# Eight chunks of the convolution's input, not four, projected during the first stage, with undivided fp32 weights

## The chip, the cores and the metric

One NeuronCore of a Trainium2 chip runs the whole program. The metric is the device time of one execution in microseconds (us), the median of the executions shown. The kernel is written in Bass with the Tile framework, which places the tiles, inserts the semaphores and orders the instructions of each engine.

## The reference

Two transformer-like blocks work on 256 tokens of width 2048. The change lies in the opening of the first block:

```python
mod = (cond @ ada_w + ada_b)                 # cond: 2048, ada_w: 2048 x 12288
sh1, sc1, g1, sh2, sc2, g2 = split(mod, 6)
h = rms_norm(x, norm_mix) * (1.0 + sc1) + sh1
proj = h @ w_in                              # q, kv, gates, z, xbc, dt
attn = nsa_attention(q, kv, gates, ...)      # 16 heads
xbc = silu(causal_depthwise_conv(xbc, conv_w, conv_b))   # 1536 channels
ssm = ssd_scan(xbc, dt, ...) * silu(z)
x = x + g1 * (concat(rms_norm(attn), ssm) @ w_out)
x = x + g2 * peer_ffn(...)
```

An entry of `sh1` or `sc1` needs all 2048 rows of its column of `ada_w`; the kernel reads these columns in four groups, so that `h` becomes ready quarter by quarter of its 2048 features.

## The kernel before, in words

**Layout.** Activations stand with the features on the partitions: 16 slices of 128 features, 256 tokens each. Weights come in tiles of 128 x 1024 fp32, 512 KB each. One chunk is 128 output columns of `w_in`; a pair of chunks is 256 columns. The 1536 channels of the convolution are 12 chunks, or 6 pairs.

**Split and whole.** A product in higher precision is made of three fp32r products: `wt` loads a weight tile into a `raw` buffer (L263: four buffers `raw` and two `rawm`) and divides it into `whi` (ScalarE, L281) and `wlo` (VectorE, L285); `mm3` (L298) multiplies high by high, high by low and low by high (L300, L301, L302). `whi` and `wlo` have two buffers each. `whole` (L290) instead loads a tile straight into a buffer of the tags `whi` or `wlo`, in turn, for one plain fp32 product; the compiler issues that as two TensorE instructions. Every one of these loads is issued on SP's queue.

**First stage.** A background generator (`mods`, L518) reads four groups of 16 tiles of `ada_w` (a quarter each; `ada`, L355) and accumulates each on VectorE (L364). After a quarter `mod` (L503) sums over the partitions on TensorE (L376), adds the bias (L508), and `chunks_T` turns four slices of `x` and writes them as `hh` and `hl`, the two parts of `h`. `early` (L561) is the foreground: for each quarter it takes 6 tiles for `kv` and `q`, accumulated over the four quarters in PSUM, and `NP` tiles for `NP` pairs of the convolution's chunks. A pair's sum over one quarter goes to a PSUM bank (tag `sm`, two banks in this stage) and is added to `part` in SBUF (L589, L591); after the last quarter `ev` of `ssd_front` applies the convolution. In quarters 0 to 2 the pairs are spread among the six, in quarter 3 they come last.

**Pacing.** `fill` (L1412) advances the foreground by one weight tile, and then the background by `bgr` steps, 16 / (NP + 5) here. `until` and `drain` call `fill` in a loop.

**Behind it.** `mixer` waits for the second `kv` tile, runs `compress` (with six calls of `fill` in it, at a `bgr` of 0.6), drains `early`, and feeds the queue with `t320` (6 tiles), the remaining chunks of the convolution (`cm`, L1338, two tiles each, `mm3`), and 16 tiles for `z`. `weave` (L1441) runs the 16 attention heads two at a time and calls `fill` at a rate of 0.28 a step. Behind the heads come 32 tiles of `w_out` (`tm_whole`, L1378, through `whole`) and the scan. Meanwhile the background reads 96 more tiles of `ada_w` (`ada_rest`, L606) at a `bgr` of 1.3; what is left of it is run off before the second half of the block.

Of the kernel before, what the change touches and what calls it, by code (L numbers as in the profile page):

```python
# [18 lines left out]
S = 256  # L19
NK = D // 128  # L20
EPS = 1e-6
LAG = 3
NP = 2

# [207 lines left out]
class K:  # L234
# [219 lines left out]
        if lo is not None:  # L454
            nc.vector.scalar_tensor_tensor(lo, ps, scale, hi.bitcast(F32), op0=ALU.mult, op1=ALU.subtract)

    def chunks_T(self, pool, x, cs, dg, hh, hl, scale, shift):

        nc = self.nc
        for c0 in range(cs[0], cs[-1], 2):  # L460
            v = self.t(pool, [128, 2, S], tag="cT", bufs=2 if dg is None else 4)
            ps = self.bank()
            for i in range(2):
                c = c0 + i
                o = ps[:, i * S : i * S + S]
                for q in range(2):
                    self.turn(o[:, q * 128 : q * 128 + 128], x[:, q, c * 128 : c * 128 + 128], None if dg is None else dg[:, q])
                if i:
                    nc.vector.tensor_scalar(v[:, i], o, scale[:, c : c + 1], shift[:, c : c + 1], op0=ALU.mult, op1=ALU.add)  # L469
                else:  # L470
                    nc.scalar.activation(v[:, i], o, AF.Identity, scale=scale[:, c : c + 1], bias=shift[:, c : c + 1])
            k = slice(c0, c0 + 2)
            self.hilo(hh[:, k], hl[:, k], v)

    def block1(self, upto=99):
        nc, tc, A = self.nc, self.tc, self.A
        con = self.con
        self.psum(6, 2)
        scr = tc.alloc_tile_pool(name="scr", bufs=1, space=DRAM)
        hp = self.hp = tc.alloc_tile_pool(name="hp", bufs=1)  # L480
        self.more = tc.alloc_tile_pool(name="more", bufs=1)
        mx = tc.alloc_tile_pool(name="mx", bufs=1)
        ax = tc.alloc_tile_pool(name="ax", bufs=1)
        xp = tc.alloc_tile_pool(name="xp", bufs=1, side="right")
        xt = self.t(xp, [128, 2, D])
        self.zeros = self.t(ax, [128, 128], F32R)
        nc.vector.memset(self.zeros.bitcast(F32), 0.0)
        self.cond = self.t(con, [128, 16])
        self.silu_small(con, self.cond, self.cp("c"), 16)
        modA = self.t(con, [128, 32])  # L490
        self.modB = self.t(con, [128, 32])
        hT = self.pair(hp, NK, "hh")
        hh, hl = hT[:2]
        cA = self.t(con, [128, 16])

        kvT = self.t(ax, [128, 4, S])
        qT = self.t(ax, [128, 8, S])
        xs, ev = self.ssd_front(mx)
        part = self.t(ax, [128, NP, 512])
        self.feed(self.early(A["w1e"], hT, kvT, qT, part, ev))  # L500
        quarter = lambda m, c: m.rearrange("p (m c j) -> p m c j", m=2, c=4)[:, :, c]

        def mod(acc, c):  # L503
            ps = self.bank()
            self.ada_mm(acc, ps[:, :8])
            yield
            p = ps[:, :8].rearrange("p (m j) -> p m j", m=2)
            nc.vector.tensor_tensor(quarter(modA, c), p, quarter(self.cp("ada_b")[:, :32], c), op=ALU.add)  # L508
            hs = slice(4 * c, 4 * c + 4)
            sc = slice(16 + 4 * c, 20 + 4 * c)  # L510
            nc.vector.scalar_tensor_tensor(cA[:, hs], modA[:, sc], 1.0, self.cp("norm_mix")[:, hs], op0=ALU.add, op1=ALU.mult)
            for i in range(2):
                k = 4 * c + 2 * i
                self.chunks_T(xp, xt, range(k, k + 2), None, hh, hl, cA, modA)
                yield
            self.done.add(("h", c))

        def mods():  # L518
            post = iter(())
            for c in range(4):  # L520
                acc = self.t(xp, [128, 1024], tag="ada", bufs=2)
                for _ in self.ada(acc, c):
                    yield
                    next(post, None)
                post = mod(acc, c)
            for _ in post:
                yield

        self.bg = [mods()]
        for _ in range(10):  # L530
            self.step_bg()
        for q in range(2):
            nc.sync.dma_start(xt[:, q], A["x"][q * 128 : q * 128 + 128])
        ss = self.t(xp, [128, 4])
        for n in range(4):
            junk = self.t(xp, [128, 2, S], tag="cT", bufs=2).rearrange("p a b -> p (a b)").bitcast(mybir.dt.bfloat16)
            x = xt[:, n // 2, n % 2 * 1024 : n % 2 * 1024 + 1024]
            nc.scalar.activation(junk, x, AF.Square, accum_out=ss[:, n : n + 1])
        sv = ss.rearrange("p (q h) -> p q h", h=2)
        nc.vector.tensor_tensor(sv[:, :, 0], sv[:, :, 0], sv[:, :, 1], op=ALU.add)  # L540
        r = self.rstd(xp, sv[:, :, 0], 2, float(D))
        for n in range(4):
            x = xt[:, n // 2, n % 2 * 1024 : n % 2 * 1024 + 1024]
            nc.scalar.activation(x, x, AF.Copy, scale=r[:, n // 2 : n // 2 + 1])
        for _ in range(6):
            self.step_bg()
        self.pack(mx, "cp2")
        self.pack(mx, "ca")
        self.bgr = 16 / (NP + 5)
        self.fill(8)  # L550
        self.bias_front(ax, scr)
        self.until(("h", 3))
        self.dbg("hh", hh.bitcast(F32))
        xp.release()
        hT = self.mixer(hp, mx, ax, hT, kvT, qT, xs, ev, scr)
        if upto < 4:
            hp.release()
            return
        return self.peer(hp, hT, upto)

    def early(self, wd, hT, kvT, qT, part, ev):  # L561

        nc = self.nc
        ps = [self.t(self.acc, [128, 512], tag="acc") for _ in range(6)]
        for p in ps:
            z = self.zeros[:, None, :].to_broadcast([128, 4, 128])
            nc.tensor.matmul(p, self.zeros, z, start=True, stop=False)
        for c in range(4):
            order = [*range(NP, NP + 6), *range(NP)]
            if c < 3:  # L570
                order.sort(key=lambda n: (n - NP) / 6 if n >= NP else (n + 0.5) / NP)
            for n in order:
                hi, lo = self.wt(wd[(NP + 6) * c + n])
                yield
                while ("h", c) not in self.done:
                    self.step_bg()
                pn = ps[n - NP] if n >= NP else self.bank()
                for i in range(2):
                    o = pn[:, i * 256 : i * 256 + 256]
                    for k in range(4):  # L580
                        sl = slice(i * 512 + k * 128, i * 512 + k * 128 + 128)
                        kk = 4 * c + k
                        if n >= NP:
                            self.mm3(o, hi[:, sl], lo[:, sl], hT[0][:, kk], hT[1][:, kk], False, kk == 15 and i == 1)
                        else:
                            self.mm3(o, hi[:, sl], lo[:, sl], hT[0][:, kk], hT[1][:, kk], k == 0, k == 3)
                if n < NP:
                    if c == 0:
                        nc.scalar.activation(part[:, n], pn, AF.Copy)  # L589
                    else:  # L590
                        nc.vector.tensor_tensor(part[:, n], part[:, n], pn, op=ALU.add)  # L591
                    if c == 3:
                        for i in range(2):
                            ev((2 * n + i + 8) % 12, part[:, n, i * 256 : i * 256 + 256])
                    continue
                if c < 3:
                    continue
                n -= NP
                o = pn.rearrange("p (a t) -> p a t", a=2)
                if n < 2:  # L600
                    nc.scalar.activation(kvT[:, 2 * n : 2 * n + 2], o, AF.Copy)
                else:
                    nc.scalar.activation(qT[:, 2 * n - 4 : 2 * n - 2], o, AF.Copy, scale=-0.125)
                self.done.add(("early", n))
# [10 lines left out]
    def mixer(self, hp, mx, ax, hT, kvT, qT, xs, ev, scr):  # L615
        nc, tc, A = self.nc, self.tc, self.A
        hh, hl = hT[:2]
# [35 lines left out]
        nc.scalar.activation(gate, vtm[:, :, 256:304], AF.Tanh, scale=0.5)  # L653
        nc.vector.tensor_scalar(gate, gate, 0.5, 0.5, op0=ALU.mult, op1=ALU.add)
        self.side.append(self.ssd_steps(mx, xs, vtm))
        at = self.t(ax, [128, 2, 1024])
        self.weave([self.head(ax, j, kv, qT, kvT, kc, vc, vtm, gate, at) for j in range(8) for kv in range(2)], 1, 0.28)
        self.dbg("attn", at)
        ss = self.t(ax, [128, 2])
        for q in range(2):  # L660
# [83 lines left out]
    def bias_group(self, ax, g):  # L744
# [4 lines left out]
        for kv in range(2):  # L749
            skew = bass.AP(tensor=ud.tensor, offset=ud.offset + 384 * (8 * kv + 2 * g), ap=[[1, 128], [384, 2], [1, 256]])  # L750
            nc.sync.dma_start(tf[:, 2 * kv : 2 * kv + 2], skew)
        tab = self.t(ax, [128, 4, 256], tag="tab", bufs=2)
        for i in range(2):
            ps = self.bank()
            nc.tensor.matmul(ps, flip, tf[:, 2 * i : 2 * i + 2], start=True, stop=True)
# [1583 lines left out]
```

## Time and profile before

| | |
|---|---|
| median of 3 executions | 3599.55 us (3596.58 to 3600.33) |
| profiled execution | 3600.31 us, its span 3598.2 us |
| mean granted TensorE clock | 0.979 of full speed |
| TensorE busy | 3427.4 us (95%) |
| VectorE, ScalarE busy | 2565.5 us (71%), 1632.8 us (45%) |
| DMA over the span | 710.40 MB, 197 GB/s |

The span is the time from the first to the last instruction of the profiled execution. A busy share is that of recorded instructions. TensorE's instructions overlap and their ends are modelled, so its pace is read from one start to the next, not from the durations.

### The profile page before, as it was taken

The page shows a single profiled execution, that of the slowest core. Times are in us where ns is not written, and L with a number is a line of the kernel's source. Part 1 is how long each engine was busy: PE and PEld are TensorE (multiplying, and loading weights), DVE is VectorE, ACT ScalarE, POOL GpSimd, SP SyncE. Part 2 cuts the span into 40 slices and gives each one's busy share as a digit, 9 for nine tenths or more (in the row PEclk, how much of TensorE's full clock was granted, in tenths as well). Part 3 has the DMA queues.
Part 4 walks back from the last instruction along what each step waited for, and adds up shares of the span by engine and source line. Part 5 has one row for each costly group of instructions (what it writes and reads, how often), then busy time and mean ns, then how long its engine had stood idle before and what let it go on. Part 6 is the DMA issues. An engine that isn't in the chain of part 4 may idle for free. (4 is left out here: it accounts for less than half of the span.)

```text
span 3598.2 us, 52389 instructions
## 1 busy us (share of the span) xinstructions
PE 3427.4 (95%) x18918; PEld 2852.2 (79%) x18918; DVE 2565.5 (71%) x4648; ACT 1632.8 (45%) x2934; POOL 390.3 (11%) x487
## 2 busy tenths in 40 slices
PE   5899999999999999999999998988999999999998
PEld 4888747888998888888878786776788888778887
DVE  7777666788887655565577658878777767666765
ACT  2355424444554444445555554333444444434444
POOL 0000010000000000000000002333223222021310
PEclk7999999999999999999999999999999999999999
DMA  9966785666456855566788765645533443434455
GB/s 345 333 222 206 266 290 177 199 198 201 159 162 208 257 185 186 187 203 205 240 271 287 254 206 186 203 160 180 169 113 113 150 138 108 134 123 159 146 182 186
DMA packets 237294, 710.40 MB, mean 197 GB/s; under 512 B 34091, under 2 KB 61804, under 8 KB 235756
## 3 DMA queue, kind: packets, MB, share of 16 engines
q1 hardware_dynamic: 207564, 672.08, 56.8%
q10 hardware_dynamic: 29472, 34.98, 2.9%
q8 instruction: 149, 2.44, 0.3%
q14 instruction: 109, 0.89, 0.1%
HBM read 673.87 MB, written 32.55 MB: 196 GB/s over the span
## 5 line engine op out<-in xcount | busy, mean ns | idle before, releaser
L285 DVE TENSOR_TENSOR wlo<-raw,whi 128x1024 fp32r<-128x1024 f32 (+1 forms) x951 | 1167.8, 1229 | 567.1 <-ACT whi L281 562.8
L281 ACT ACTIVATE whi<-raw 128x1024 fp32r<-128x1024 f32 (+1 forms) x951 | 994.0, 1046 | 1224.8 <-PE acc L302 577.3
L308 PE MATMUL acc<-hh,whi 128*128 128x512 f32 x3328 | 1197.9, 401 | 0.7 <-DVE cT L469 0.7
L309 PE MATMUL acc<-hh,wlo 128*128 128x256 f32 x3328 | 940.0, 282 | 7.1 <-DVE wlo L285 6.9
L308 PEld LDWEIGHTS acc<-hh,whi 128*128 128x128 f32 x3328 | 627.0, 188 | 145.6 <-issue 4.5
L309 PEld LDWEIGHTS acc<-hh,wlo 128*128 128x128 f32 x3328 | 629.6, 189 | 13.5 <-DVE wlo L285 12.0
L301 PE MATMUL acc<-wlo,wh 128*128 128x512 f32 x1024 | 402.1, 393 | 8.0 <-DVE wlo L285 7.2
L300 PE MATMUL acc<-whi,wh 128*128 128x512 f32 x1024 | 396.6, 390 | 3.5 <-DVE ge L1355 2.8
L302 PE MATMUL acc<-whi,wl 128*128 128x512 f32 x1024 | 399.3, 390 | 0.0
L301 PE MATMUL acc<-wlo,hh 128*128 128x512 f32 (+1 forms) x608 | 243.7, 401 | 14.9 <-DVE wlo L285 14.7
L300 PE MATMUL acc<-whi,hh 128*128 128x512 f32 (+1 forms) x608 | 248.1, 409 | 5.3 <-DVE r L1355 5.3
L302 PE MATMUL acc<-whi,hh 128*128 128x512 f32 (+1 forms) x608 | 242.1, 398 | 0.0
L301 PEld LDWEIGHTS acc<-wlo,wh 128*128 128x128 f32 x1024 | 192.5, 188 | 58.6 <-DVE wlo L285 18.8
L300 PEld LDWEIGHTS acc<-whi,wh 128*128 128x128 f32 x1024 | 192.3, 188 | 45.7 <-ACT wh L281 3.1
L302 PEld LDWEIGHTS acc<-whi,wl 128*128 128x128 f32 x1024 | 192.7, 188 | 38.9
L302 PE MATMUL acc<-hh,wlo 128*128 128x256 f32 x608 | 181.7, 299 | 27.9 <-DVE wlo L285 27.9
L300 PE MATMUL acc<-hh,whi 128*128 128x256 f32 x608 | 182.3, 300 | 5.4 <-ACT whi L281 3.4
L301 PE MATMUL acc<-hh,whi 128*128 128x256 f32 x608 | 178.5, 294 | 1.0 <-DVE hh L285 1.0
L301 PEld LDWEIGHTS acc<-wlo,hh 128*128 128x128 f32 x608 | 118.3, 195 | 43.1 <-DVE wlo L285 21.1
L302 PEld LDWEIGHTS acc<-hh,wlo 128*128 128x128 f32 x608 | 122.0, 201 | 34.0 <-DVE wlo L285 31.9
L1819 POOL TENSOR_TENSOR r<-r,cb 128x256 f32<-128x256 f32 x144 | 129.7, 920 | 163.7 <-DVE r L2149 38.1
L364 DVE SCALAR_TENSOR_TENSOR ada<-raw,u,ada 128x1024 f32<-128x1024 f32 x101 | 131.7, 1304 | 21.6 <-DMA raw<-in_ada_dram 20.7
(591 smaller groups left out, 4913.8 us busy)
## 6 DMA issues: line engine op xcount, KB each, us to landing
raw<-in_pu_dram SPq DMA_DIRECT2D x256, 512.0 KB, 3.6
raw<-in_pv_dram SPq DMA_DIRECT2D x252, 512.0 KB, 4.2
raw<-in_ada_dram SPq DMA_DIRECT2D x139, 512.0 KB, 5.2
raw<-in_w2gate_dram SPq DMA_DIRECT2D x96, 512.0 KB, 3.6
rawm<-in_ada_dram SPq DMA_DIRECT2D x53, 512.0 KB, 5.5
raw<-in_w2br_dram SPq DMA_DIRECT2D x48, 512.0 KB, 3.5
raw<-in_w2g_dram SPq DMA_DIRECT2D x48, 512.0 KB, 3.5
raw<-in_wq_dram SPq DMA_DIRECT2D x32, 512.0 KB, 3.6
```

The lines of the kernel that those rows point to most:

```text
L281: nc.scalar.activation(hi, src, AF.Copy)
L285: self.lo = e.tensor_sub(lo, src, hi.bitcast(F32)).ins
L300: mm(out, shi, mhi, start=start, stop=False)
L301: mm(out, shi, mlo, start=False, stop=False)
L302: mm(out, slo, mhi, start=False, stop=stop)
L308: mm(out, hi, both, start=start, stop=False)
L309: mm(out[:, S:], lo, both[:, 0], start=False, stop=stop)
L364: nc.vector.scalar_tensor_tensor(acc, w, c, acc, op0=ALU.mult, op1=ALU.add)
L1819: PL.tensor_tensor(v2(lb), v2(L), cb(f"M{b}"), op=ALU.mult)
```

## The change

`NP` goes from 2 to 4. The pairs no longer use `wt` and `mm3`: their weight tile is loaded by `whole`, and multiplied in plain fp32 with an undivided `h`, which `chunks_T` now leaves in a tile `v` for a whole quarter. That tile takes a buffer of the tag `tab` (three buffers now, two before; the attention's bias tables use the same tag later), and `part` shares its buffer with `at`, the attention's output. `w1cm`, the array for `cm`, has 8 tiles fewer, `w1e` 8 more. `bgr` in the first stage becomes 16/9 from 16/7, and the rate in `weave` goes from 0.28 to 0.23.

```diff
-NP = 2
+NP = 4
...
-    def chunks_T(self, pool, x, cs, dg, hh, hl, scale, shift):
+    def chunks_T(self, pool, x, cs, dg, hh, hl, scale, shift, v=None):
...
-            v = self.t(pool, [128, 2, S], tag="cT", bufs=2 if dg is None else 4)
+            if dg is not None:
+                v = self.t(pool, [128, 2, S], tag="cT", bufs=4)
...
-        part = self.t(ax, [128, NP, 512])
-        self.feed(self.early(A["w1e"], hT, kvT, qT, part, ev))
+        part = self.t(ax, [128, 2048], tag="at").rearrange("p (n t) -> p n t", n=NP)
+        parts = {}
+        self.feed(self.early(A["w1e"], hT, parts, kvT, qT, part, ev))
...
+            v = parts[c] = self.t(ax, [128, 4, S], tag="tab", bufs=3)
...
-                self.chunks_T(xp, xt, range(k, k + 2), None, hh, hl, cA, modA)
+                self.chunks_T(xp, xt, range(k, k + 2), None, hh, hl, cA, modA, v[:, 2 * i : 2 * i + 2])
...
-                hi, lo = self.wt(wd[(NP + 6) * c + n])
+                if n < NP:
+                    w = self.whole(wd[(NP + 6) * c + n])
+                else:
+                    hi, lo = self.wt(wd[(NP + 6) * c + n])
...
-                            self.mm3(o, hi[:, sl], lo[:, sl], hT[0][:, kk], hT[1][:, kk], k == 0, k == 3)
+                            nc.tensor.matmul(o, w[:, sl], parts[c][:, k], start=k == 0, stop=k == 3)
...
-        at = self.t(ax, [128, 2, 1024])
-        self.weave([...], 1, 0.28)
+        at = self.t(ax, [128, 2048], tag="at").rearrange("p (q c) -> p q c", q=2)
+        self.weave([...], 1, 0.23)
...
-        tab = self.t(ax, [128, 4, 256], tag="tab", bufs=2)
+        tab = self.t(ax, [128, 4, 256], tag="tab", bufs=3)
```

## Rows read from the trace of the kernel before

**Rows 1.** The page: span, and DMA share in tenths in 40 slices.

```profile
span 3598.2 us, 52389 instructions
...
DMA  9966785666456855566788765645533443434455
```

**Rows 2.** Stages: length, busy time (instructions) per engine, clock, DMA share, GB/s.

```profile
36.50:69.50 33.00, 25.82 (x170) 23.23 (x169) 28.78 (x29) 9.13 (x11) 0.00 (x0) 0.81 0.95 344
69.50:105.70 36.20, 27.91 (x196) 24.86 (x195) 30.94 (x32) 10.07 (x12) 0.00 (x0) 0.95 0.90 331
105.70:141.10 35.40, 28.32 (x194) 26.98 (x192) 31.11 (x32) 9.59 (x11) 0.00 (x0) 0.86 0.97 350
141.10:182.00 40.90, 37.72 (x279) 35.91 (x277) 24.02 (x29) 16.88 (x22) 0.00 (x0) 0.92 0.89 301
182.00:224.30 42.30, 40.91 (x287) 37.74 (x287) 29.87 (x46) 18.83 (x31) 0.40 (x4) 0.92 0.75 253
224.30:314.00 89.70, 89.42 (x657) 79.94 (x656) 72.59 (x233) 52.82 (x166) 5.12 (x16) 0.98 0.62 193
314.00:403.20 89.20, 89.20 (x500) 73.27 (x500) 64.64 (x187) 45.48 (x144) 4.68 (x8) 0.92 0.61 197
```

**Rows 3.** Line L508, the bias behind each of the four quarters.

```profile
L508 DVE TENSOR_TENSOR u<-sm,cp x4: 166/167/168, 36.5 to 141.1; 128x8 f32<-128x8 f32 x4
```

**Rows 4.** Line L267 from 36.5 to 141.1 us: SP's issues and landings.

```profile
L267 SPq DMA_DIRECT2D raw<-in_ada_dram x30: 327/328/332, 40.3 to 137.6; - x30
L267 SPq DMA_DIRECT2D raw<-in_w1e_dram x15: 327/328/351, 38.0 to 136.4; - x15
L267 SPq DMA_DIRECT2D rawm<-in_ada_dram x14: 327/328/383, 38.7 to 129.4; - x14
L267 SPq DMA_DIRECT2D rawm<-in_w1e_dram x9: 327/328/328, 51.7 to 138.9; - x9
...
DMA to landing us min/median/max: 3.6/5.3/7.0
```

**Rows 5.** Timeline of TensorE: first matmuls of two adjoining divided tiles.

```profile
151.27 0.28 PE L300 MATMUL acc<-hh,whi 128*128 128x256 f32 x1
...
154.09 0.28 PE L300 MATMUL acc<-hh,whi 128*128 128x256 f32 x1
```

**Rows 6.** Timeline of TensorE from 504 to 562 us, whole tiles of `w_out`.

```profile
504.76 3.60 PE L1387 MATMUL acc<-whi,hh 128*128 128x512 f32 x8
508.19 0.60 PE L441 MATMUL sm<-cs,u 128*128 128x128 f32 x4
...
560.82 1.40 PE L376 MATMUL sm<-ones,ada 128*128 128x1 f32 x12
```

**Rows 7.** Timeline of SP: issue of a `w1e` tile.

```profile
122.63 0.33 SPq L267 DMA_DIRECT2D raw<-in_w1e_dram  x1
```

**Rows 8.** Timeline of VectorE: a division, a `part` sum.

```profile
130.37 1.22 DVE L285 TENSOR_TENSOR wlo<-raw,whi 128x1024 fp32r<-128x1024 f32 x1 [1.03 <-ACT whi L281]
...
134.58 0.69 DVE L591 TENSOR_TENSOR u<-u,sm 128x512 f32<-128x512 f32 x1 [0.47 <-PE sm L302]
```

**Rows 9.** Timeline of SP from 504 to 545 us.

```profile
504.95 0.33 SPq L295 DMA_DIRECT2D wlo<-in_wo_dram  x1
505.37 0.38 SPq L267 DMA_DIRECT2D raw<-in_ada_dram  x1
508.39 0.33 SPq L295 DMA_DIRECT2D whi<-in_wo_dram  x1
...
541.21 0.91 SPq L267 DMA_DIRECT2D raw<-in_wq_dram  x2
```

**Rows 10.** Timeline of VectorE: the background's last sum.

```profile
549.50 1.28 DVE L364 SCALAR_TENSOR_TENSOR ada<-raw,u,ada 128x1024 f32<-128x1024 f32 x1
```

**Rows 11.** A stage of `w_out` and the scan; columns as in rows 2.

```profile
416.00:436.00 20.00, 20.00 (x76) 11.44 (x76) 13.57 (x19) 7.25 (x17) 0.00 (x0) 1.00 1.02 406
```

More of the change, by code (lines that the diff above doesn't have):

```diff
@@ L559, in block1, with early @@
         return self.peer(hp, hT, upto)
-    def early(self, wd, hT, kvT, qT, part, ev):
+    def early(self, wd, hT, parts, kvT, qT, part, ev):
         nc = self.nc
@@ L655, in mixer @@
         self.side.append(self.ssd_steps(mx, xs, vtm))
-        at = self.t(ax, [128, 2, 1024])
-        self.weave([self.head(ax, j, kv, qT, kvT, kc, vc, vtm, gate, at) for j in range(8) for kv in range(2)], 1, 0.28)
+        at = self.t(ax, [128, 2048], tag="at").rearrange("p (q c) -> p q c", q=2)
+        self.weave([self.head(ax, j, kv, qT, kvT, kc, vc, vtm, gate, at) for j in range(8) for kv in range(2)], 1, 0.23)
         self.dbg("attn", at)
```

## The prediction

> **What bounds the kernel now.** I read the page first, for its DMA line: the first two of 40 slices, each 90 us of the span, are the only ones in which the DMA engines are at nine tenths [rows 1]. The table of stages then shows that the opening has two parts with different limits [rows 2]. In the first, which I bound by the bias of quarters 0 and 3 at 36.5 and 141.1 us [rows 3], the DMA share is 0.90 to 0.97 and TensorE has records in only about 77 to 80% of the time, although each record's end is stretched by the model. In the second, from 182 us on, TensorE is full and the DMA share falls to 0.75 and, under the attention heads (224.3 to 403.2 us), to 0.61. So work moved from behind the heads' start into the first part trades TensorE time for DMA time. The stretch between, 141.1 to 224.3 us, belongs to neither: TensorE is at 92 to 97%, at a granted clock of 0.92, and DMA at 0.75 to 0.89.
>
> Line L267 gives the first part's pace [rows 4]: 30 + 15 + 14 + 9 = 68 tiles issued in 104.6 us, 1.54 us each, and a median of 5.3 us from issue to landing, so some 3.4 tiles are in flight.
>
> Two more prices. A divided tile (24 matmuls of 256 columns) takes TensorE 154.09 - 151.27 = 2.82 us [rows 5]. A plain fp32 tile is not in this stage, but the tiles of `w_out` are: eight instructions of 512 columns, 508.19 - 504.76 = 3.43 us [rows 6]. A pair's tile is 16 instructions of 256 columns, the same number of columns with the same pass over each, so I take 3.43 us.
>
> **The change part by part.** *TensorE's total.* Removed: 8 divided tiles of the two old pairs in the first stage and 8 divided tiles of four chunks in `cm`, 16 x 2.82 = 45.1 us. Added: 16 whole tiles, 16 x 3.43 = 54.9 us. The sum rises by 9.8 us, so the change can only gain by filling time in which TensorE idles. Where this falls matters.
>
> *First part, up to quarter 3's bias.* The counters of the code fix how many `w1e` tiles are issued before `h` is complete: the background needs 68 steps, 20 are done by the second `fill`, and 48 / (16/7) = 21 further ones follow, 22 tiles of 32. With 16/9 it is 48 / (16/9) = 27, 28 tiles of 40. Six more tiles at 1.54 us are +9.2 us if DMA stays the limit. TensorE would carry about 17 divided and 11 whole tiles there, 48 + 38 = 86 us, with the turns and sums (some 10 us) under 100 of 114 us: it has room. VectorE loses eight divisions of 1.22 us in the whole stage and gains six sums of 0.69 us [rows 8]: room too (90.8 us busy of 104.6 before, [rows 2]).
>
> *The whole tile's wait.* This is new. `whole` writes into a `whi` or `wlo` buffer, so SP may issue it only when TensorE is done with that buffer's last tile, and behind it on SP's queue stand all the `raw` loads, the `ada_w` tiles among them. I followed the two buffers of each tag through the order kv/q, pair, kv/q, kv/q, pair, q, pair, q, q, pair: pairs 0 and 2 of a quarter wait for the tile three places back, pairs 1 and 3 for the one two places back. From issue to the end on TensorE a divided tile takes 130.37 - 122.63 = 7.7 us to the start of `wlo`, 1.22 for it and 2.82 of matmuls, 11.8 us [rows 7, 8, 5]. Places are 114 / 28 = 4.1 us apart. Three places (12.2 us) need no wait; two (8.1 us) make SP wait about 3.7 us. That the queue really goes in step with TensorE in such a case is seen at `w_out`: SP issues whole tiles at 504.95 and 508.39, each 0.2 us behind a step of TensorE at 504.76 and 508.19, and the `ada_w` loads only behind them [rows 9, 6]. The cover is what is in flight: 5.3 us. While it lasts, a 3.7 us wait costs DMA nothing; without it the full 3.7 us. Six such waits: 0 to 22 us. I take 2.5 us, near the covered end, since the wait is shorter than the flight.
>
> *Middle part, up to the heads.* Before, 10 divided tiles are left (28.2 us). After, 12: the last divided one and the last pair of quarter 2, then six divided and four whole, 7 x 2.82 + 5 x 3.43 = 36.9 us, +8.7 us. TensorE has few gaps here, so I count it in full. The four pairs now come last, and the evacuation of pairs 2 and 3 stands on ScalarE and VectorE ahead of `t320`'s first divisions: 0 to 4 us, taken as 1.
>
> *Heads and behind.* Eight divided tiles of `cm` go, 22.6 us, at full price because TensorE is full [rows 2]. Against it: the heads keep their latencies and get 0.23/0.28 of the filler. The granted clock under the heads is 0.98 and 0.92; read as a mix of its two levels, 2.4 and 1.2 GHz, that is 0.04 x 89.7 + 0.16 x 89.2 = 18 us at the lower one, which costs some 9 us. With less filler between small matmuls this could double, with luck vanish: -9 to +9, taken as +2, since of these two rows the one with fewer matmuls (500 against 657) has the lower clock.
>
> *At nothing.* Eight fewer calls of `fill` behind `early`'s end leave some eight background tiles to the end of the block: 0.6 x 11 + 1.3 x 70 = 98 steps before, 0.6 x 11 + 1.3 x 64 = 90 after. They are issued where SP now takes up the next loads, 541.21 us, and need 8 x 1.54 = 12 us; the last sum is now done at 549.5 and would be at about 556, under the last `w_out` tiles, which end at 560.82 [rows 6, 9, 10]. Cover left 5 us; without it, up to 8. The two buffers shared (`part` with `at`, `v` with the bias tables) are free long before their next owner. The `sm` banks hold twice as many pairs, with a 2.82 us tile between two of them against a 0.69 us sum.
>
> **The sum.** +9.2 + 2.5 + 8.7 + 1 - 22.6 + 2 = +0.8 us on the profiled 3600.31, 3601.1. The median lies 0.8 us below that execution, so 3600.3; I say 3600.5.
>
> **The rivals.** A measurement of this kernel can tell some 0.2%, 7.2 us, from no change.
>
> *SP's wait starves DMA (slower).* If the flight is shorter than the wait each of six waits costs its 3.7 us, less what I counted: 22 - 2.5 = +19.5, 3620. For it: the wait is worked out from a single tile's 11.8 us and grows with every delay of TensorE. Against it: the 5.3 us in flight. It decides from about 1.6 us a wait.
>
> *The heads lose their clock (slower).* The 18 us at the lower level double: +9 for +2, 3607.5 and up to 3612 with `t320` late by 4. For it: the 0.92 of the second half. Against it: 0.98 in the first.
>
> *DMA has more to give (faster).* From 416 to 436 us the same tiles come at 406 GB/s [rows 11], against 331 to 350 in the first part. At 406 a 512 KB tile takes 1.29 us, 74 tiles 95 us: DMA would no longer set this part and it would stay at 104.6 us, -9.2 and no stall: 3589. Against it: the DMA engines are already 0.90 to 0.97 busy there, so the bytes per busy time are lower, not the queue idle.
>
> The Trainium skill, Perfetto Trace Analysis, section Roofline, puts the practical ceiling of a single core at about 120% of its 358 GB/s, some 430 GB/s. By that the first part would not be limited by DMA at all, as in this rival; the busy share in this trace speaks against it, and the 406 GB/s of rows 11 for it.
>
> *The middle stretch and the heads gain clock (faster).* From 141.1 to 224.3 us the clock of 0.92 is 0.08 x 2 x 83.2 = 13 us at the lower level, worth 6.5 us; with that back and no loss under the heads, 3592, and less if the heads gain as well.
>
> **How the numbers follow.** My own case, all terms near those taken, 0.42, between 3592.4 and 3606.8. SP's wait 0.18, the heads' clock 0.12; DMA 0.13, clock gained 0.15. So faster by over 0.2% is 0.28, within 0.42, slower 0.30. The range of 8 in 10 leaves out the far half of SP's wait and of DMA's ceiling: 3588 to 3614.
>
> **What would show it.** Quarter 3's bias near 153 us and the heads' first VectorE instruction near 246 us, against 224.3; the last head's sum about 181 - 14 us behind the first. SP's wait: gaps between issues longer than 5 us ahead of whole tiles, and a DMA share under 0.85 before quarter 3's bias. The clock: granted clock under the heads below 0.90. The prediction is wrong if the first part grows by less than 6 or more than 18 us, or if the heads' stretch shortens by much less than its share of filler.

## The result, and the profile after

The changed kernel takes 3621.53 us, median of 6 runs (3603.67 to 3631.02), and the kernel before, on the same chip, 3598.14 us (3595.57 to 3601.13, 6 runs): a ratio of 1.0058, with an interval of 1.0036 to 1.0080. The change makes the kernel slower by some 0.6%. Forecast were 3600.5 us, and no difference as the likeliest.

The profiled execution took 3623.8 us. Its page, the lines that answer to [rows 1]; PEclk is TensorE's granted clock in tenths of full speed:

```profile
span 3622.0 us, 52097 instructions
...
PEclk7989999999999999999999999999999999999999
...
DMA  8865676666545855566688765545533443434455
```

The DMA share of the first two slices fell from nine tenths and more to eight. The marks that bound the stages, with line, operation, count, durations, and first and last start: the four quarters' bias (it answers to [rows 3]), the heads' first VectorE instruction, the heads' sums.

```profile
L510 DVE TENSOR_TENSOR u<-sm,cp x4: 160/166/168, 37.0 to 153.0; 128x8 f32<-128x8 f32 x4
...
L845 DVE CUSTOM_DVE_ANT_0 s<-sm,tab x96: 145/290/425, 262.9 to 417.3; 128x128 f32<-128x128 f32 x32, 128x256 f32<-128x256 f32 x32, 128x7 f32<-128x7 f32 x16, 128x15 f32<-128x15 f32 x16
...
L892 DVE TENSOR_REDUCE at<-ow x16: 552/589/596, 276.3 to 426.1; 128x128 f32<-128x384 f32 x16
```

I cut both traces at the same five marks: quarter 0's bias, quarter 3's bias, the heads' first VectorE instruction, the end of the last head's sum, the end of the last sum behind `w_out`. The windows between them have the columns of [rows 2]: stretch, length, busy time of TensorE, its weight loads, VectorE, ScalarE, GpSimd, then granted clock, DMA share, GB/s. Kernel before:

```profile
36.50:141.10 104.60, 82.05 (x556) 75.07 (x555) 90.83 (x91) 28.79 (x34) 0.00 (x0) 0.88 0.94 342
141.10:224.30 83.20, 78.64 (x564) 73.65 (x563) 53.88 (x74) 35.71 (x53) 0.40 (x4) 0.92 0.82 277
224.30:403.20 178.90, 178.62 (x1154) 153.21 (x1154) 137.23 (x419) 98.30 (x309) 9.80 (x24) 0.95 0.62 195
403.20:563.50 160.30, 157.68 (x537) 83.67 (x535) 101.15 (x129) 43.99 (x99) 24.00 (x17) 1.00 0.83 297
```

Kernel after:

```profile
37.00:153.00 116.00, 100.93 (x596) 88.31 (x596) 88.69 (x89) 25.60 (x32) 0.00 (x0) 0.91 0.85 324
153.00:262.90 109.90, 97.09 (x617) 88.71 (x617) 64.19 (x96) 37.47 (x66) 2.85 (x10) 0.89 0.74 254
262.90:426.70 163.80, 163.74 (x964) 136.51 (x964) 117.80 (x390) 87.73 (x287) 6.08 (x18) 0.93 0.55 173
426.70:587.90 161.20, 156.03 (x504) 81.25 (x502) 102.23 (x129) 41.53 (x97) 20.12 (x17) 0.96 0.83 295
```

The span grew by 23.8 us: +0.5 ahead of quarter 0's bias, +11.4 in the first part, +26.7 in the middle stretch, -15.1 under the heads, +0.9 behind them, -0.6 from there to the end. What comes after 588 us is as long in both traces (3034.1 and 3034.7 us). Over the 20 traces of this document it runs from 3025.1 to 3041.5 us, though no edit changes the code there, so a few microseconds between two single traces are not a finding by themselves. Two rows say more than their lengths. Under the heads TensorE has records in 163.74 of 163.80 us, at a granted clock of 0.93 (a mix of its two levels, 2.4 and 1.2 GHz): a busy share of 100% that is not TensorE at full rate. As the ends of the records are modelled, the row does not say whether short gaps lie between them. And behind the heads it has fewer matmuls (504 for 537), yet takes as long, since idle time and clock took what was saved.

I use one measure for this below. The work of a stretch is TensorE's busy time times the granted clock, and its loss is the length less that work. Before, the losses of the middle stretch, the heads and the stretch behind are 83.2 - 78.64 x 0.92 = 10.9, 9.2 and 2.6 us; after, 23.5, 11.5 and 11.4. The work is 72.3, 169.7 and 157.7 before and 86.4, 152.3 and 149.8 after. The clock is a mean over the whole row, so the split is rounded by a microsecond or two. In the first part the measure fails (the same instructions give 72.2 us of work before and 77.4 in f1 below), and I don't use it there.

What fills the middle stretch: the lines of TensorE from 153.0 to 262.9 us (matmuls, their busy sum and mean, idle time just before them).

```profile
L795 PE MATMUL sm<-Y,cw 128*128 128x30 f32 x128 | 18.6, 307 | 5.9 <-DMA cw<-in_cw_dram 5.9
L593 PE MATMUL sm<-tab,whi 128*128 128x256 f32 x48 | 13.4, 442 | 1.0 <-DMA whi<-in_w1e_dram 1.0
L593 PE MATMUL sm<-tab,wlo 128*128 128x256 f32 x48 | 11.2, 383 | 1.7 <-DMA wlo<-in_w1e_dram 1.7
...
L376 PE MATMUL sm<-ones,ada 128*128 128x1 f32 x16 | 1.8, 245 | 0.0
...
L924 PE MATMUL sm<-cs,cvs 128*128 128x128 f32 x8 | 1.5, 276 | 0.0
```

L593 is a pair's tile in plain fp32, 16 records each: 96 records, six tiles. The same view of before has three pair tiles there. The longest gap, on TensorE's timeline (start, duration, instruction):

```profile
221.12 7.04 PE L795 MATMUL sm<-Y,cw 128*128 128x30 f32 x32 [5.38 <-DMA cw<-in_cw_dram]
228.08 6.10 PE L593 MATMUL sm<-tab,whi 128*128 128x256 f32 x16
```

TensorE stood for 5.38 us for the third quarter of the compression's weights, and the whole tile behind it took 6.0 us to the next matmul instead of the 3.3 to 3.7 us that such tiles take in the first part: the granted clock was 0.50 from 221.1 to 228.1 us and 0.60 from 228.1 to 234.1. The second half of the compression, in slices of 10 us, with the columns of the windows above:

```profile
213.00:223.00 10.00, 4.62 (x34) 4.51 (x34) 7.13 (x12) 3.22 (x7) 0.20 (x2) 0.64 0.81 287
223.00:233.00 10.00, 10.00 (x37) 8.96 (x37) 2.81 (x3) 0.39 (x2) 0.00 (x0) 0.50 0.50 155
```

Here lie 20.0 - (4.62 x 0.64 + 10.00 x 0.50) = 12.0 of the 23.5 us that the middle stretch loses. Before, no 10 us of that stretch have a clock below 0.80.

### The profile page after: what moved, and what is told of

Same layout as the page of the kernel before. It is cut to its first block, busy times and chain, and to the rows that moved or that the text cites. A ratio compares the mean times of both kernels' runs of the same rounds, so it can differ in the third digit from the quotient of the medians.

```text
span 3622.0 us, 52097 instructions
## 1 busy us (share of the span) xinstructions
PE 3448.8 (95%) x18790; PEld 2861.3 (79%) x18790; DVE 2555.3 (71%) x4638; ACT 1618.1 (45%) x2920; POOL 385.5 (11%) x487
## 5 line engine op out<-in xcount | busy, mean ns | idle before, releaser
L309 PE MATMUL acc<-hh,wlo 128*128 128x256 f32 x3328 | 939.5, 282 | 8.8 <-DVE wlo L285 8.8
L309 PEld LDWEIGHTS acc<-hh,wlo 128*128 128x128 f32 x3328 | 628.9, 189 | 14.6 <-DVE wlo L285 13.5
L301 PE MATMUL acc<-wlo,hh 128*128 128x512 f32 (+1 forms) x608 | 243.5, 401 | 16.1 <-DVE wlo L285 15.9
L301 PEld LDWEIGHTS acc<-wlo,wh 128*128 128x128 f32 x1024 | 192.9, 188 | 56.9 <-DVE wlo L285 16.8
L302 PE MATMUL acc<-hh,wlo 128*128 128x256 f32 x544 | 164.7, 303 | 22.0 <-DVE wlo L285 21.9
L300 PE MATMUL acc<-hh,whi 128*128 128x256 f32 x544 | 165.0, 303 | 2.7 <-ACT hh L281 2.0
L301 PE MATMUL acc<-hh,whi 128*128 128x256 f32 x544 | 161.2, 296 | 1.0 <-DVE hh L285 1.0
L301 PEld LDWEIGHTS acc<-wlo,hh 128*128 128x128 f32 x608 | 117.0, 192 | 44.7 <-DVE wlo L285 22.9
L300 PEld LDWEIGHTS acc<-whi,hh 128*128 128x128 f32 x608 | 116.9, 192 | 34.5 <-issue 11.6
```

The costliest lines, as they stand in the source:

```text
L300: mm(out, shi, mhi, start=start, stop=False)
L301: mm(out, shi, mlo, start=False, stop=False)
L302: mm(out, slo, mhi, start=False, stop=stop)
L309: mm(out[:, S:], lo, both[:, 0], start=False, stop=stop)
```

## The experiments

All runs stand against the kernel before on the same chip. Times are medians with the lowest and the highest; the losses are from one profiled execution of each.

### First round: is it the whole tiles' wait, the plain matmuls, or the move?

Theory A of these four is the rival of the prediction that SP's wait for `whi` or `wlo` blocks what stands behind it; B that the added work is the cost; C that it is the move with its pacing and clock.

**e1_raw_pairs**, the changed kernel, pairs' tiles in the buffers of the raw loads:

```
-                    w = self.whole(wd[(NP + 6) * c + n])
+                    w = self.raw(wd[(NP + 6) * c + n])
```

> The pair's undivided tile is loaded into a raw buffer and multiplied from there, not into a whi or wlo buffer; the plain fp32 product stays. Theory A (SP's wait for a whi or wlo buffer holds up the loads behind it in the middle stretch, with ScalarE and the loads of cw1 behind these): the stretch from quarter 3's bias to the heads falls from 109.9 us to under 98, the total to 3600 to 3608 us. Theory B (the added work itself, five whole tiles and four more evacuations, makes the stretch long): it stays at 106 to 112 us, the total at 3617 to 3625. Theory C (the move and its pacing, fewer calls of fill and a lower clock): as B.

3619.94 us (3616.37 to 3631.08), ratio 1.0054, interval 1.0033 to 1.0075. The first part is 116.2 us long against 116.0, the middle stretch 107.9 against 109.9. But the edit moves the wait and does not remove it: a `raw` buffer that holds a pair's tile also comes free only when TensorE is done with it. What SP waited for in the first part (in all, times, longest, in us), in the changed kernel:

```profile
SPq L295 <- PE acc L301: 19.0, 5, 5.8
...
SPq L295 <- DVE wlo L285: 10.0, 4, 3.9
SPq L295 <- PE acc L302: 6.4, 5, 2.9
```

and in e1:

```profile
SPq L267 <- PE sm L593: 24.2, 9, 4.4
```

So this run does not test a kernel without the wait; e3 does.

**e2_cw_gpsimd**, the changed kernel, with the compression's weights issued from another queue, since ScalarE, which issues them, stood for 5.2 us for a `w1t` tile just before:

```
-                nc.scalar.dma_start(w1, A["cw1"][i, :, 1024 * r : 1024 * r + 1024])
+                nc.gpsimd.dma_start(w1, A["cw1"][i, :, 1024 * r : 1024 * r + 1024])
```

> The loads of cw1 for compress are issued by GpSimd, not ScalarE; all else as after. Theory A, in the form that ScalarE, held up by a late t320 tile, issues cw1 late: the longest gap before a matmul of compress falls from 5.66 us to under 1.5, the clock between 210 and 235 us stays high, and the total falls by 6 to 12 us, to 3610 to 3616. Theory B and C: no change within 3 us.

3627.48 us (3614.16 to 3632.74), 1.0062, interval 1.0041 to 1.0084. No gain; TensorE's gap for these weights is 7.29 us in its trace.

**e3_divided_np4**, the changed kernel with the pairs' tiles divided as before (four pairs, shared buffers):

```
-                if n < NP:
-                    w = self.whole(wd[(NP + 6) * c + n])
-                else:
-                    hi, lo = self.wt(wd[(NP + 6) * c + n])
+                hi, lo = self.wt(wd[(NP + 6) * c + n])
...
-                            nc.tensor.matmul(o, w[:, sl], parts[c][:, k], start=k == 0, stop=k == 3)
+                            self.mm3(o, hi[:, sl], lo[:, sl], hT[0][:, kk], hT[1][:, kk], k == 0, k == 3)
```

> Four pairs in the first stage, but divided and with three fp32r products as before the change. No whole tile is left there. Theory A: SP never waits for TensorE, the middle stretch is 83 us plus two divided tiles and two pairs' evacuations, 90 to 95 us, total 3592 to 3602. Theory B (plain fp32 passes): TensorE loses 16 x 0.61 = 9.8 us, so 3608 to 3614. Theory C (the move): still 3615 or more.

3617.67 us (3613.08 to 3626.95), 1.0043, interval 1.0028 to 1.0058. Without any plain matmul the kernel is nearly as slow. Its first part is 118.0 us long and its middle stretch 107.4, with no whole tile there for SP to wait for, so at four pairs the wait is not what makes the kernel slow.

**e4_whole_np2**, the changed kernel with two pairs (`NP = 2`, 0.28):

> Two pairs in the first stage, as before, but with whole tiles and plain fp32; rate of weave 0.28, background 16/7. Theory A: two whole tiles in quarter 3 hold up SP once or twice: 3 to 10 us over before. Theory B: TensorE gains 8 x 0.61 = 5 us, most of it under DMA: 1 to 2 us over before. Theory C: no change.

3623.59 us (3616.08 to 3634.02), 1.0061, interval 1.0038 to 1.0083. With nothing moved it is just as slow. Neither the move nor the plain tiles alone explain both runs; so I looked for what e3 and e4 have in common, the shared buffers.

### Second round: the shared buffers, the move alone, the middle stretch

From here on theory C is the shared buffers, B the plain tiles, M the move itself.

**f1_np2_shared**, the kernel before with the shared buffers alone:

```
-        part = self.t(ax, [128, NP, 512])
+        part = self.t(ax, [128, 2048], tag="at")[:, :1024].rearrange("p (n t) -> p n t", n=NP)
...
+            v = self.t(ax, [128, 4, S], tag="tab", bufs=3)
...
-        tab = self.t(ax, [128, 4, 256], tag="tab", bufs=2)
+        tab = self.t(ax, [128, 4, 256], tag="tab", bufs=3)
```

> The kernel before (two pairs, divided tiles, 0.28) with the buffers alone of the change: a quarter's v as one tile of three shared with the bias tables, part and at in one buffer. Together with e4_whole_np2, which differs from it only in the plain fp32 tiles, it splits e4's +22 us. Theory C (the shared buffers make h late or the tables wait): 3612 to 3622, quarter 3's bias later than 145. Theory B (the plain tiles themselves: 8 of them x 0.61 us on TensorE, and SP's wait for their buffers): 3597 to 3604, quarter 3's bias near 141.

3600.11 us (3588.44 to 3611.92), 0.9995, interval 0.9979 to 1.0012. The shared buffers cost nothing, as predicted.

**f2_np4_alone**, the kernel before with four pairs and 0.23, nothing else:

```
-NP = 2
+NP = 4
...
-        self.weave([...], 1, 0.28)
+        self.weave([...], 1, 0.23)
```

> The kernel before with four pairs and 0.23 and nothing else of the change: divided tiles, v and part in buffers of their own. It differs from e3_divided_np4 only in the shared buffers. Theory C: 3596 to 3604. Theory M (the move itself: TensorE has three pair tiles more behind quarter 3's bias, of which two come only after the compression, and idles in the compression): 3613 to 3620, middle stretch 105 to 109 as in e3.

3618.85 us (3612.71 to 3632.55), 1.0053, interval 1.0034 to 1.0073. The move alone costs nearly as much as the whole change. Its windows, from quarter 0's bias on:

```profile
36.50:151.40 114.90, 94.15 (x677) 86.55 (x677) 98.36 (x99) 35.93 (x42) 0.00 (x0) 0.97 0.93 334
151.40:256.00 104.60, 93.96 (x654) 88.37 (x653) 68.94 (x100) 43.87 (x72) 4.39 (x10) 0.87 0.74 250
256.00:426.00 170.00, 169.89 (x975) 141.37 (x976) 118.89 (x392) 87.26 (x287) 7.61 (x18) 0.90 0.53 172
426.00:583.50 157.50, 152.59 (x504) 79.70 (x502) 101.97 (x128) 41.65 (x97) 18.81 (x17) 0.98 0.85 301
```

Work was 72.3 and is 81.7 us in the middle stretch, 16.8 us less under the heads and 8.2 less behind them. The losses of these three are 22.9, 17.1 and 8.0 us, 48.0 in sum against 22.7 before. So the move takes 25 us of work from behind the heads' start and gets 11.7 us of time for it.

**f3_fill3**, the changed kernel with one tile more inside each half of the compression:

```
             self.tabs[i] = self.bias_group(ax, i)
-            self.fill(2)
+            self.fill(3)
```

> The changed kernel with three tiles instead of two between the tables and the compression's matmuls, so that all four pairs of quarter 3 stand inside the compression. Theory M: the two tiles left behind the compression now cover its waits (TensorE idled 12.8 us in the middle stretch against 4.6 before), middle stretch 100 to 104 instead of 109.8, whole 3612 to 3617. Theory B (the added work itself): no change, 3619 to 3624.

3622.14 us (3610.98 to 3631.42), 1.0059, interval 1.0038 to 1.0081. The middle stretch is 106.4 us: idle time fell from 12.8 to 7.5 us, but the clock from 0.89 to 0.87. Partly as theory M has it in the profile, nothing in the time (the traced execution, 3612.0 us, is the second lowest of the six).

**f4_no_bg_mid**, the changed kernel with the background stopped in the middle stretch:

```
-        self.bg, self.bgr = [self.ada_rest(adr)], 0.6
+        self.bg, self.bgr = [self.ada_rest(adr)], 0.0
...
-        self.bgr = 1.3
+        self.bgr = 1.45
```

> The changed kernel with the background of ada_w tiles stopped until the compression is issued (0.6 to 0) and then faster (1.3 to 1.45). Some ten 512 KB loads leave the middle stretch, which had 27.9 MB against 23.0 before. If SP's queue and the DMA set the middle stretch (the loads of w1t and w1cm wait behind ada_w): middle stretch 100 or less, whole 3608 to 3615. If TensorE's own work and the compression's chain set it: middle within 3 us of 109.8, whole 3619 to 3626.

3622.09 us (3612.62 to 3631.51), 1.0058, interval 1.0040 to 1.0077; middle stretch 109.3 us at 220 instead of 254 GB/s. So the transfers that were taken out don't set its length.

### Third round: the number of pairs, the compression's weights, the heads' rate

**g1_np1** and **g2_np3**, the kernel before with one pair (0.305) and with three (0.255), divided tiles:

> The kernel before with one pair in the first stage instead of two (0.305 for 0.28), divided tiles, buffers as before; ten chunks stay in cm. Theory M (each pair moved forward costs more ahead of the heads than it gives back under and behind them; two more pairs alone cost 16.7 us): by the same ledger the other way 3592 to 3598, quarter 3's bias near 136, middle stretch near 73. Rival S (two pairs are a flat optimum, and below it the compression loses its cover): 3602 or more, with TensorE's idle time in the middle stretch over 8 us.

> The kernel before with three pairs (0.255), divided tiles, buffers as before. Theory M: half of the loss of four pairs, 3608 to 3613, middle stretch 92 to 96. Rival S (a step: the fourth pair's tiles no longer fit into the compression): 3600 to 3605, middle stretch near 88.

One pair: 3606.89 us (3601.04 to 3624.05), 1.0029, interval 1.0014 to 1.0043. Three: 3595.15 us (3589.30 to 3604.23), 0.9991, interval 0.9980 to 1.0001. Theory M as a straight line falls with both: three pairs cost nothing, and one is slower. Rival S gets the time of one pair right, but not for its reason: TensorE idles 2.5 us in the middle stretch, not over 8. Three pairs are faster than both ranges had it. The windows of three pairs, middle stretch, heads and behind:

```profile
144.80:238.40 93.60, 87.29 (x608) 81.06 (x609) 59.87 (x86) 39.03 (x62) 0.60 (x6) 0.89 0.77 262
238.40:403.60 165.20, 163.78 (x1063) 138.11 (x1062) 129.18 (x407) 94.17 (x300) 10.72 (x22) 0.99 0.62 192
403.60:562.70 159.10, 155.62 (x522) 81.73 (x520) 102.03 (x130) 42.29 (x98) 17.78 (x17) 0.99 0.84 302
```

The middle stretch is 10.4 us longer than before and the heads 13.7 shorter. With more filler left than four pairs leave (1063 matmuls under the heads against 975) the heads are 4.8 us shorter than in f2, at a clock of 0.99 instead of 0.90.

**g3_fill3_cw3**, f3 with a third buffer for the compression's weights:

```
-                w1 = self.t(cp, [128, 1024], tag="cw1", bufs=2)
+                w1 = self.t(cp, [128, 1024], tag="cw1", bufs=3)
```

> f3_fill3 with three buffers instead of two for the compression's weights, so that their third load need not wait for TensorE. In f3 TensorE waited 3.62 us for that load and its clock then stood at half. If the gap and the clock behind it are the loss of the middle stretch: middle 98 to 101 against 106.3, whole 3610 to 3616. If the added work is what it costs: middle 104 or more, whole 3618 to 3624.

3626.66 us (3621.62 to 3634.53), 1.0072, interval 1.0059 to 1.0086. TensorE's waits for these weights fell from 4.6 us in f3 to 1.3, and the middle stretch stays at 106.5 us, at a clock of 0.86 (0.53 and 0.61 from 195.1 to 215.1 us, 0.58 from 235.1 to 245.1, about the compression's matmuls). The gap alone is not the loss.

**g4_rate28**, the changed kernel with the heads' filler at 0.28:

```
-        self.weave([...], 1, 0.23)
+        self.weave([...], 1, 0.28)
```

> The changed kernel with the heads' filler at 0.28, as before, instead of 0.23. If the give-back is lost because filler is missing behind the heads (idle 4.6 us and 6.6 us of clock from 426 to 587 us against 2.1 and 0): more is missing there now, heads' stretch 168 to 172, whole 3622 to 3628. If the heads lack filler (11.9 us of clock under them against 8.5): whole 3612 to 3618.

3634.30 us (3631.66 to 3638.52), 1.0095, interval 1.0082 to 1.0108. Losses 22.4 us under the heads and 15.9 behind, the time above both ranges. The filler runs out before the heads end: in their last 35.8 us each of the three products of the divided filler tiles has 8 matmuls (in the last 33.7 us of the changed kernel's heads 22 or 23), at a clock of 0.75. The new rate of the change is worth some 13 us to it.

### Fourth round: rate or number of chunks; the plain tiles again

**h1_np3_rate23** is g2 at 0.23, **h2_np4_rate255** is f2 at 0.255.

> g2_np3 (three pairs, divided) with the heads' filler at 0.23 instead of 0.255. Theory R (the loss under the heads is the thinner filler: below some rate TensorE's granted clock falls, 16.9 us of it with four pairs at 0.23, 1.7 with three at 0.255): clock lost under the heads 8 us or more, heads' stretch 170 or more, whole 3600 to 3608. Theory N (it is the number of chunks left, not the rate): clock lost under 4 us, whole 3594 to 3598.

> f2_np4_alone (four pairs, divided) at 0.255 instead of 0.23. Theory R: clock lost under the heads back to 5 us or less, heads' stretch 158 to 163, whole 3606 to 3613 (the middle stretch stays). Theory N: clock lost stays over 10 us and the filler ends sooner, whole 3620 to 3628, like g4_rate28 against the changed kernel.

h1: 3605.65 us (3600.79 to 3614.03), 1.0017, interval 1.0007 to 1.0027. h2: 3617.85 us (3613.01 to 3628.89), 1.0051, interval 1.0035 to 1.0067. Heads and the stretch behind, of h1:

```profile
240.40:408.90 168.50, 168.48 (x1038) 140.99 (x1037) 121.24 (x401) 92.21 (x297) 9.47 (x22) 0.93 0.53 167
408.90:575.50 166.60, 163.65 (x551) 87.91 (x550) 108.15 (x135) 44.65 (x100) 18.57 (x17) 0.98 0.85 308
```

and of h2:

```profile
261.50:425.10 163.60, 160.91 (x989) 133.36 (x989) 125.92 (x398) 89.62 (x289) 7.15 (x18) 0.98 0.63 203
425.10:589.00 163.90, 155.93 (x488) 80.57 (x488) 91.75 (x122) 41.10 (x95) 17.64 (x17) 0.93 0.75 266
```

With the rate alone the heads' clock goes from 0.99 to 0.93 at three pairs and from 0.90 to 0.98 at four: theory R has the direction right. At three pairs the times show it too (the intervals of g2 and h1 do not overlap). At four pairs it is less sure: the eight traces with four pairs at 0.23 lose 6.7 to 17.1 us under the heads, so f2 is the far end and h2's 5.9 lies just below them. Nor does the rate alone set the clock: two pairs at 0.28 have 0.94 to 0.97 (before, f1, e4, h4), less than three at 0.255. And at four pairs nothing is won: the heads' loss falls from 17.1 to 5.9 us and that of the stretch behind rises from 8.0 to 18.9. The sum is 25 us at both rates. I read it so that four pairs leave too few chunks to fill both stretches.

**h3_change_np3**, the whole change with three pairs and 0.255; **h4_raw_np2**, e4 with the pairs' tiles in the raw buffers, as in e1.

> The whole change (plain fp32, whole tiles, shared buffers) with three pairs and 0.255 instead of four and 0.23. It differs from g2_np3 by the plain tiles and the shared buffers, of which the latter cost nothing with two pairs. If the plain tiles cost what they did with two pairs (22 us): 3612 to 3618. If they cost what they do with four (3 us): 3596 to 3602.

> e4_whole_np2 with the pairs' tiles in the buffers of the raw loads instead of whi and wlo, so that SP need not wait for TensorE. Theory A at two pairs (SP's wait is e4's cost): 3600 to 3606, quarter 3's bias back from 147.7 to 143 to 144. Otherwise (the plain matmuls): 3616 to 3624.

h3: 3614.85 us (3608.49 to 3617.14), 1.0037, interval 1.0023 to 1.0050. h4: 3615.79 us (3609.45 to 3624.40), 1.0043, interval 1.0028 to 1.0058. So plain tiles cost some 17 to 20 us at three pairs as well. Like e1, h4 does not take SP's wait away: SP waited 13.4 us in four places for L593 in its first part, which is as long as e4's (110.9 us in h4, 110.5 in e4, 106.3 in f1). So what the wait costs with two pairs is not settled.

### Fifth round: is there a better rate?

**k1_np3_rate28** is the kernel before with `NP = 3` alone; **k2_np2_rate31** is the kernel before with 0.31 for 0.28 and nothing else.

> The kernel before with three pairs and the heads' filler left at 0.28 (g2_np3 has 0.255, h1 0.23). Theory R with a fixed amount of filler: the heads keep their clock (under 4 us lost), but the chunks run out sooner and the stretch behind the heads loses more than g2's 3.2 us idle and 1.7 us of clock, as four pairs did from 0.23 to 0.255 (4.8 and 3.4 to 7.4 and 9.9): 3597 to 3606. If three pairs have enough for both: 3590 to 3596, which would be the best version.

> The kernel before with 0.31 instead of 0.28 and nothing else. Theory R: it has the filler of two more chunks than three pairs leave, so the heads lose less clock (8.5 us before, to under 4) and the stretch behind loses at most a few us: 3592 to 3600. If the filler behind the heads is as scarce as with three pairs at 0.28: 3602 to 3608.

k1: 3611.04 us (3605.86 to 3615.50), 1.0028, interval 1.0017 to 1.0039. k2: 3592.11 us (3589.29 to 3600.24), 0.9976, interval 0.9964 to 0.9989. Heads and behind, of k2:

```profile
223.30:401.70 178.40, 178.40 (x1202) 155.93 (x1201) 146.65 (x429) 101.82 (x313) 11.94 (x24) 0.99 0.68 217
401.70:556.50 154.80, 151.05 (x487) 77.03 (x485) 92.03 (x120) 41.56 (x97) 19.08 (x17) 0.98 0.79 282
```

The heads do 6.9 us more work than before in 0.5 us less, at 0.99, and the stretch behind is 5.5 us shorter. k2 is the only version here that beats the kernel before, and both kernels of the study.

All kernels with divided tiles, as losses of the traced execution (us), with the time of that execution and the median; f1 and e3 have the shared buffers besides:

| kernel | pairs, rate | middle | heads | behind | sum | traced us | median us |
|---|---|---|---|---|---|---|---|
| k2 | 2, 0.31 | 9.6 | 1.8 | 6.8 | 18.2 | 3591.43 | 3592.11 |
| f1 | 2, 0.28 | 12.0 | 6.7 | 1.4 | 20.1 | 3600.94 | 3600.11 |
| before | 2, 0.28 | 10.9 | 9.2 | 2.6 | 22.7 | 3600.31 | 3598.14 |
| g2 | 3, 0.255 | 15.9 | 3.1 | 5.0 | 24.0 | 3593.37 | 3595.15 |
| g1 | 1, 0.305 | 9.2 | 6.1 | 9.1 | 24.4 | 3601.39 | 3606.89 |
| h1 | 3, 0.23 | 14.7 | 11.8 | 6.2 | 32.7 | 3611.93 | 3605.65 |
| k1 | 3, 0.28 | 13.0 | 4.3 | 16.6 | 33.9 | 3607.19 | 3611.04 |
| f2 | 4, 0.23 | 22.9 | 17.1 | 8.0 | 48.0 | 3614.44 | 3618.85 |
| h2 | 4, 0.255 | 26.4 | 5.9 | 18.9 | 51.2 | 3620.30 | 3617.85 |
| e3 | 4, 0.23 | 26.5 | 13.5 | 11.8 | 51.8 | 3617.53 | 3617.67 |

before and f1, and f2 and e3, are nearly the same program: they show that such a loss differs by up to 4 us from trace to trace.

## Why the prediction was wrong, point by point

**First part: right in size, in part by luck.** +11.4 us, predicted 9.2 + 2.5. SP issued 63 raw and 10 whole tiles between the two biases, 73 where 74 were predicted, 1.59 us each. The five tiles more are 7.7 us at the old pace of 1.54; the rest is the slower pace. But the 2.5 us for SP's wait are not shown: with divided tiles alone (f2) the same 73 tiles take 114.9 us, 1.57 each.

**The wait as a rival: it is there, but not its price.** SP waited 35.4 us for `whi` and `wlo` buffers, in 14 places of up to 5.8 us, where six of 3.7 were predicted, and the DMA share of 0.85 stands at the bound named as a sign (0.80 to 0.88 in the ten kernels with plain tiles, 0.90 to 0.94 in the ten with divided ones). At four pairs the part is yet no longer than with divided tiles (114.9 in f2, 118.0 in e3), where SP waits instead for VectorE to free the `raw` buffers (82.4 us in f2). So f2 and e3, not e1, refute the 19.5 us of this rival at four pairs. At two and three it is open (below).

**DMA has more to give: its forecast did not come.** The part did not stay at 104.6 us. As SP waits for buffers through most of it in every version, no run shows how fast DMA could be there.

**Middle stretch: the step that failed.** +26.7 us, predicted 8.7 + 1. The prediction named no sign for this stretch of its own except the heads' start near 246 us (measured 262.9), and its two signs of being wrong, on the first part and on the heads, did not show. Two things were missing. The work rose by 14.1 us, not 9.7: I counted two tiles more behind quarter 3's bias, there were three pair tiles more, so six plain tiles (3.3 to 3.7 us each, against the 3.43 predicted) in place of three divided ones, and 3.3 us of the background's and the scan's small matmuls (L376, L924), almost absent there before, came ahead of the heads. And the loss rose from 10.9 to 23.5 us: "TensorE has few gaps here, so I count it in full" took it that added tiles bring no gaps and no lower clock. Half of the loss lies about the second half of the compression, at a clock of 0.50 to 0.64. Less of the named gap (f3, g3) brought 3.5 us of the stretch back, fewer transfers (f4) 0.6. That the loss grows with the number of pairs is shown (9 to 12 us for one and two, 13 to 16 for three, 23 to 27 for four, divided); why the clock falls so far about the compression and the loss jumps at the fourth pair is not.

**Heads and behind: the other part of the miss.** Predicted 22.6 - 2 = 20.6 us back, got 15.1 - 0.9 = 14.2. The mark named, 14 us off the heads, was met, but the rest, due behind the heads, did not come. The work fell by 17.4 and 7.9 us, 25.3 in all; the losses of both stretches rose by 11.1. The rival of the clock was right in kind: h1 against g2 shows it with nothing changed but the rate. It looked only under the heads, though, while the stretch behind lives on the same chunks. In f2 and h2 the rate chooses only which of the two pays.

The Trainium skill, TensorE: Matmul & The Clock Gate, Part 1, says that TensorE's clock is throttled by default and that its activity releases it. These traces are in line with it: under the same heads 0.93 at a rate of 0.23 and 0.99 at 0.255 with three pairs, 0.90 and 0.98 with four. The Trainium skill's Perfetto Trace Analysis, Identifying the Most-Contended Engine, warns that TensorE's matmul busy time is a bad measure of how near its limit a kernel is; here the heads show 100% busy in h1 and in k2, at 0.93 and at 0.99.

**At nothing: right, as far as the runs can tell.** The shared buffers cost nothing (f1). The background's last sum starts at 576.5 us, under the last `w_out` tiles, whose last sum ends at 587.9. From there to the end the span is 3034.1 us after and 3034.7 before, an agreement closer than the 16 us by which this time varies over the traces.

**The sum.** The first part was off by -0.3 us, the middle stretch by +17.0, heads and behind by +6.4; with that 0.8 becomes 23.9, against 23.8 in the two traces (23.4 between the medians).

**Open.** The plain tiles cost 15 to 24 us at two and three pairs (e4 and h4 against f1, h3 against g2), and at four some 3 us, inside the intervals (the change against f2, e3). Counted by TensorE's work they are 0.6 us a tile, 8 tiles at two pairs. In the traces the cost is spread: of h3 against g2, 11.6 us are in the first part, of e4 against f1, 4.2 there, 2.6 in the middle, 5.9 under the heads and 4.3 behind, and 5.3 in the part that no edit touches. For the first part SP's wait is an untested rival: h3 issued 69 tiles at 1.72 us each against 71 at 1.51 in g2, SP waited 44.6 us for `whi` and `wlo` buffers, up to 7.8 at once, and the DMA share was 0.80 against 0.93. No run has plain tiles whose buffers SP need not wait for, so the wait is not told from the other effects of a plain tile. The costs of the change's parts don't add up, and no run here says why.

## What to carry to other kernels

Work that is moved forward is also filler that is taken away: before counting a tile's full time as a gain, look at what is left to fill every stretch that it filled, and multiply busy time by granted clock, since a busy share of 100% hides a slow clock. When the number of filler tiles changes, their rate has to be tried anew, for all stretches that share them at once. And an edit with two parts needs both run alone: here each alone (f2, e4) costs the 0.5 to 0.6% that the two cost together. An experiment that takes a wait away has to be checked in its own trace: e1 and h4 only moved it to another buffer.

## What the runs showed that I had not expected

One constant of the order of work, the heads' filler rate, moves the kernel by 9 to 13 us for 0.025 (three pairs, against the kernel before on the same chip: 0.9991 at 0.255, 1.0017 at 0.23, 1.0028 at 0.28), while a third pair with a rate of its own makes no difference clear of noise (g2). TensorE's granted clock fell to 0.93 in a stretch in which its records, whose ends are modelled, leave no gap (168.48 of 168.50 us in h1).
